# An 8-tap causal convolution on one core: H0 takes over a row sum of H1, and half of an H1 output moves from VectorE to ScalarE and GpSimd

## The chip, the core and the metric

The kernel runs on one core of a Trainium2 chip. The metric is the device time of one execution in microseconds (us). The kernel before takes 728.31 us, the median of three runs (727.57 to 728.33). The execution that the profiler recorded took 728.58 us, and its span, from the first to the last instruction of the program, is 726.8 us; 1.78 us lie around the span.

## The reference

```
out = zeros_like(x)                       # x: (8, 4096, 512), kernel: (8, 512, 512), float32
for k in range(8):
    shifted = x if k == 0 else concat([zeros((B, k, D)), x[:, :-k, :]], axis=1)
    out += matmul(shifted, kernel[k])
```

Each output row is the sum of eight products of 512x512 matrices with the present row of x and the seven before it.

## The kernel before

**Layout.** The 8 x 4096 rows are cut into 128 runs of 256 rows, one run for each partition. A "row" below is one time step t of all 128 runs: a tile of 128 x 512. The first four rows are computed directly; the other 252 are computed in 21 blocks of 12.

**The algorithm.** The eight taps are three bits, and on each bit a product of two 2-part sums is replaced by three products instead of four. So a block has four *nodes*: PL, MI, H1 and H0 (numbers k = 4m+1 to 4m+4 in block m). A node forms sums of rows of x, multiplies them with sums of taps (the W tiles), and gives four output rows in two halves, LO and HI, of two rows each. The outputs of a block are H1's sums (rows t to t+3), the middle sums (t+4 to t+7, out of PL and MI), and H0's (t+8 to t+11).

**The steps of a node**, by the names that the order list uses (the digit after the dot says which node: .0 to .3 are PL, MI, H1 and H0 of the block, .4 to .6 the first three of the next; in s0, s1, v0, v1, d0, d1, F0, F1, e0, e1 the last digit is the half, in l00 to l11 the half and the row):

- z (VectorE): seven sums or differences of rows of XR into Z, 128 x 3584 in one instruction or 1536 + 2048 in two where the ring of 20 rows wraps. H0 takes three of its seven from H1 and computes four (128 x 2048).
- A (VectorE): two sums of neighbouring Z rows (128 x 1024). PL and H1 keep Z in rows 0 to 6 of the tile and their A in rows 9 and 10; MI and H0 keep Z in rows 4 to 10 and their A in rows 0 and 1.
- s (VectorE): five sums of Z rows two apart into S (128 x 2560). F0, F1 (VectorE): two sums each of neighbouring S rows (128 x 1024).
- a1, u, a0 (TensorE): products with A and Z into the PSUM pair q; after a1 ScalarE copies one bank of q onto the other, and a0 waits for that.
- s0, s1 (ScalarE): the seeds, copies of q into the two PSUM pairs p[LO] and p[HI]; dt (ScalarE): a copy of q into DT in SBUF.
- v0, v1 (TensorE): products with S onto the seeds; d0, d1 (VectorE): p[.][0] = DT minus p[.][1] and the like; l00 to l11 (TensorE): products with F onto both rows.
- e0, e1: the ends. For PL two ScalarE instructions, for MI, H1 and H0 one VectorE instruction of 128 x 1024 that reads PSUM and a y tile; H1's and H0's ends are followed by a store. ga, gb (GpSimd): halves of the middle sums, 128 x 512 f32 each, then a store.

Every product is four matmuls of 128 x 128 by 128 x 512, so a block has 36 products, 144 matmuls. The PSUM pairs of p go round by three, the y tiles are five buffers.

**The order of the work** is written out by hand: a prologue line by line (`go`, `do`, `wsum`, ...), then the list ORDER once for each block. Each engine executes its own steps strictly in this order; semaphores keep the dependences between engines. `behind` makes a GpSimd instruction wait for the VectorE instruction that stands last before it in the program; GpSimd also issues the loads of x (r0 to r2), SyncE the transposes into XR (x12, x16, x20) and the stores. LATE places two weight sums of the prologue (wl, wh) at steps of the list.

**Lines.** `tt` records every VectorE tensor_tensor at line 84 and `stt` every scalar_tensor_tensor at line 87; all products have line 125; GpSimd's halves have line 276; the ScalarE copies are lines 186 (q), 202 and 204 (s0, s1), 208 (dt), 247 and 249 (PL's ends). The change touches node_s, node_F, comps, node_e, the ORDER list and LATE.

Of the kernel before, what the change touches and what calls it, by code (L numbers as in the profile page):

```python
# [8 lines left out]
LO, HI, MID = 0, 1, 2  # L9
H1, H0, MI, PL = 0, 1, 2, 3  # L10
# [4 lines left out]
def kernel(  # L15
# [6 lines left out]
    nc = tc.nc  # L22
    B, S, D = x.shape
    K = kernel.shape[0]
    P = 128
# [8 lines left out]
    ADD = mybir.AluOpType.add  # L34
    SUB = mybir.AluOpType.subtract
# [34 lines left out]
    F = spool.tile([P, 4, D], bf, name="F")  # L70
# [12 lines left out]
    def tt(o, a, b, op):  # L83
        last["dve"] = nc.vector.tensor_tensor(out=o, in0=a, in1=b, op=op)  # L84

    def stt(o, a, by, b, op):
        last["dve"] = nc.vector.scalar_tensor_tensor(out=o, in0=a, scalar=by, in1=b, op0=MUL, op1=op)  # L87
# [18 lines left out]
    def load_x(t):  # L106
        if t < RUN:
            xd[t] = dpool.tile([P, 4, D], bf, name="xd")
            return rows(xd[t], t, 4)

    def behind(i):
        tc.add_manual_dep(i.ins, last["dve"].ins.name,
                          mybir.DependencyInfo(mybir.DependencyClass.Sync, mybir.DependencyReason.DATA),
                          reason="behind")

    def transpose_x(t):
        if t < RUN:
            transpose(t, xd[t])
# [10 lines left out]
    class Node:  # L129
        def __init__(self, k, t, a):  # L130
            self.k, self.t, self.a = k, t, a
            self.z, self.o = Z, 4 if a in (MI, H0) else 0
            self.leaf = k in LEAF
            self.s = WX[:, 0:5] if k <= EARLY and k % 2 else S
            if k <= EARLY:
                self.A = WX[:, 5 + 2 * (k % 2):7 + 2 * (k % 2)]
            elif self.o:
                self.A = Z[:, 0:2]
            else:
                self.A = Z[:, 9:11]  # L140
            self.p = {}
# [20 lines left out]
    def node_A(n):  # L162
        tt(n.A, n.z[:, n.o + 2:n.o + 4], n.z[:, n.o + 3:n.o + 5], ADD)

    def node_s(n):
        tt(n.s, n.z[:, n.o:n.o + 5], n.z[:, n.o + 2:n.o + 7], ADD)

    def node_F(n, b_):
        if not n.leaf:
            s = n.s  # L170
            tt(F[:, 2 * b_:2 * b_ + 2], s[:, 2 * b_:2 * b_ + 2], s[:, 2 * b_ + 1:2 * b_ + 3], ADD)

    def comps(n):
        s, a = n.s, n.A
        return (n.z[:, n.o + 3], [a[:, 0], a[:, 1]], [s[:, j] for j in range(5)],
                [F[:, j] for j in range(4)])

    def node_a1(n):
        n.q = pair(3)
        u, a, _, _ = comps(n)  # L180
        if n.leaf:
            product(n.q[:, 1], u, W[n.a, MID, MID], True)
            nc.scalar.mul(out=n.q[:, 0], in_=n.q[:, 1], mul=-1.0)
        else:
            product(n.q[:, 1], a[1], W[n.a, MID, HI], True)
            nc.scalar.copy(out=n.q[:, 0], in_=n.q[:, 1])  # L186

    def node_a0(n):
        product(n.q[:, 0], comps(n)[1][0], W[n.a, MID, LO], False)

    def node_u(n):
        u, a, _, _ = comps(n)
        if n.leaf:
            product(n.q[:, 1], a[1], W[n.a, MID, HI], False)
        else:
            product(n.q[:, 1], u, W[n.a, MID, MID], False)
# [17 lines left out]
    def node_d(n, b_):  # L214
        if n.leaf:
            return
        p = n.p[b_]
        if b_ == LO:
            tt(p[:, 0], DT, p[:, 1], SUB)
        else:  # L220
            stt(p[:, 0], p[:, 1], -1.0, DT, SUB)
# [9 lines left out]
    def store(t, y):  # L231
        nc.sync.dma_start(out=orr[:, t:t + 2, :], in_=y)

    cc, dd = {}, {}

    def y_tile():
        return ypool.tile([P, 2, D], f32, name="y")

    def node_e(n, b_):
        p, t = n.p[b_], n.t + 2 * b_  # L240
        first = n.k <= 4
        if n.a == PL:
            cc[b_] = y_tile()
            if first:
                nc.scalar.mul(out=cc[b_], in_=p, mul=0.5)
            else:
                nc.scalar.copy(out=cc[b_], in_=p)  # L247
                dd[b_] = y_tile()
                nc.scalar.mul(out=dd[b_], in_=cc[b_], mul=-0.5)
        elif n.a == MI:  # L250
            if first:
                dd[b_] = y_tile()
                stt(dd[b_], p, -0.5, cc[b_], ADD)
            else:
                stt(dd[b_], p, 0.5, dd[b_], ADD)
        elif n.a == H1:
            y = y_tile()
            tt(y, p, dd[b_], ADD if first else SUB)
            store(t, y)
        elif n.k == len(nodes) - 1 and b_ == HI:  # L260
            for j, eng in enumerate((nc.scalar, nc.sync)):
                stt(dd[b_][:, j], dd[b_][:, j], -1.0, p[:, j], SUB)
                eng.dma_start(out=orr[:, t + 8 + j, :], in_=dd[b_][:, j])
        else:
            if first:
                tt(dd[b_], dd[b_], p, SUB)
            else:
                stt(dd[b_], dd[b_], -1.0, p, SUB)
            store(t + 8, dd[b_])

    def middle(n, b_):
        stt(cc[b_], cc[b_], 2.0, dd[b_], SUB)
        store(n.t + 4 + 2 * b_, cc[b_])
# [13 lines left out]
    def terms(a, b_, c_):  # L287
        if a == MI and b_ != MID and c_ != MID:
            return W[H0, b_, c_], W[H1, b_, c_]
        if b_ == c_ == MID:  # L290
            return W[a, MID, LO], W[a, MID, HI]
        if b_ == MID:
            return W[a, HI, c_], W[a, LO, c_]
        return W[a, b_, LO], W[a, b_, HI]

    def wsum(a, b_, c_):
        p, m = terms(a, b_, c_)
        tt(W[a, b_, c_], p, m, SUB)
# [51 lines left out]
    def direct_out(b_):  # L350
        y = y_tile()
        nc.scalar.copy(out=y, in_=pd[b_])
        store(2 * b_, y)
# [4 lines left out]
    def s_rows(n, a, b):  # L358
# [2 lines left out]
    nodes = [None] + [Node(1 + 4 * k + i, HEAD + STEP * k, a) for k in range(NB)  # L361
                      for i, a in enumerate((PL, MI, H1, H0))]
    ORDER = """
        d1.1 a0.2 s.2 e0.1 z.3 F0.2 A.3 u.2 l10.1 l11.1 ga0.2 x16.0 x20.1 dt.2 e1.1 s0.2 s1.2 v0.2 v1.2 r1.6
        d0.2 F1.2 d1.2 a1.3 l01.2 a0.3 s.3 z.4 u.3 dt.3 s0.3 l00.2 gb0.2 v0.3 e0.2 l10.2 d0.3 s1.3 F0.3
        l11.2 v1.3 F1.3 l01.3 A.4 s.4 ga1.2 gb1.2 a1.4 l00.3 e1.2 d1.3 e0.3 u.4 a0.4 s1.4 l10.3 z.5 r2.2
        l11.3 s0.4 v0.4 dt.4 v1.4 A.5 a1.5 F0.4 d0.4 r0.2 F1.4 d1.4 l00.4 s.5 e1.3 l01.4 e0.4 a0.5 u.5 s0.5
        z.6 l10.4 s1.5 l11.4 v0.5 F0.5 A.6 v1.5 dt.5 d0.5 a1.6 e1.4 l01.5 x12.4 l00.5 F1.5
    """.split()

    def rows_ahead(n, i):
        d = load_x(n.t + 3 * STEP + 4 * i)
        if d:
            behind(d)

    ACTS = {
        "z": node_z, "s": node_s, "A": node_A, "a1": node_a1, "a0": node_a0, "u": node_u,
        "F0": lambda n: node_F(n, 0), "F1": lambda n: node_F(n, 1),
        "s0": lambda n: node_seed(n, 0), "s1": lambda n: node_seed(n, 1), "dt": node_dts,
        "v0": lambda n: node_v(n, 0), "v1": lambda n: node_v(n, 1),  # L380
# [7 lines left out]
        "x12": lambda n: transpose_x(n.t + 12), "x16": lambda n: transpose_x(n.t + 16),  # L388
        "x20": lambda n: transpose_x(n.t + 20), 
        "r0": lambda n: rows_ahead(n, 0), "r1": lambda n: rows_ahead(n, 1), "r2": lambda n: rows_ahead(n, 2),  # L390
        "wl": lambda n: wsum(H0, LO, MID), "wh": lambda n: wsum(H0, HI, MID),
    }
    AHEAD = {"F0": 1, "s": 1, "z": 2, "A": 2, "a0": 1, "u": 1, "a1": 2, "b1": 1, "s0": 1, "s1": 1,
# [3 lines left out]
    def do(name, k):  # L397
        if k < len(nodes) and (name, k) not in done:
            done.add((name, k))
            ACTS[name](nodes[k])  # L400

    def go(k, name):
        do("a1" if name == "b1" else name, k + AHEAD.get(name, 0))
# [118 lines left out]
    go(3, "v1")  # L522
    node_v(nodes[1], 1)
    node_F(nodes[1], 0)
    direct_out(1)
    node_A(nodes[2])
    node_d(nodes[1], 0)
    go(2, "v0")
    node_a1(nodes[2])
    wsum(MI, MID, LO)  # L530
    wsum(MI, MID, MID)
    load_x(20)
    go(1, "l00")
    node_d(nodes[1], 1)
# [19 lines left out]
    go(1, "v0")  # L554
    go(1, "F0")
    go(2, "a0")
    go(1, "d0")
    go(2, "F1")
    go(2, "u")
# [40 lines left out]
    go(4, "l00")  # L600
    go(3, "s1")
    go(4, "b1")
    wsum(H1, LO, MID)
    go(4, "s")
    go(4, "F0")
    go(4, "l11")
    go(4, "a0")
    go(4, "e0")
    go(4, "u")
# [3 lines left out]
    go(4, "z")  # L613
    go(4, "A")
    go(4, "g1")
    do("r1", 7)
    go(4, "s0")
    go(4, "v0")
    go(4, "d0")
# [5 lines left out]
    done |= {("r0", 3), ("r1", 3), ("r2", 3)}  # L625
    done |= {(name, k) for name in ("ga0", "gb0", "ga1", "gb1") for k in (1, 2, 3, 4)}
    done |= {(name, k) for name in ("F0", "F1", "dt", "v0", "v1", "d0", "d1") for k in LEAF}
    LATE = {(0, "d1.4"): [("wl", 8)], (0, "z.6"): [("wh", 8)]}
    for m in range(NB):
        for token in ORDER:  # L630
            name, i = token.split(".")
            do(name, 4 * m + int(i) + 1)
            for late in LATE.get((m, token), ()):
                do(*late)


# [28 lines left out]
```

## Time and profile before

| what | value |
|---|---|
| median of three runs | 728.31 us |
| the profiled execution, and its span | 728.58 us, 726.8 us |
| TensorE busy (matmuls) | 701.1 us, 96% of the span |
| VectorE busy | 696.9 us, 96% |
| ScalarE busy | 277.3 us, 38% |
| GpSimd busy | 142.7 us, 20% |
| mean granted TensorE clock | 0.997 |
| DMA, mean rate | 192 GB/s |

The page gives busy time and share of each engine, the span in 40 slices, the chain of work that ended last, and groups of equal instructions with the mean duration of one and the idle time before them. Busy time is the union of the instructions' spans. The matmuls are pipelined, and so are VectorE's instructions to a small degree: a record lasts longer than the distance to the next one's start. What an instruction takes from its engine is the distance from its start to the next start, called its *slot* below.

### The profile page before, as it was taken

The page shows a single profiled execution, that of the slowest core. Times are in us where ns is not written, and L with a number is a line of the kernel's source. Part 1 is how long each engine was busy: PE and PEld are TensorE (multiplying, and loading weights), DVE is VectorE, ACT ScalarE, POOL GpSimd, SP SyncE. Part 2 cuts the span into 40 slices and gives each one's busy share as a digit, 9 for nine tenths or more (in the row PEclk, how much of TensorE's full clock was granted, in tenths as well). Part 3 has the DMA queues.
Part 4 walks back from the last instruction along what each step waited for, and adds up shares of the span by engine and source line. Part 5 has one row for each costly group of instructions (what it writes and reads, how often), then busy time and mean ns, then how long its engine had stood idle before and what let it go on. Part 6 is the DMA issues. An engine that isn't in the chain of part 4 may idle for free. (4 is left out here: it accounts for less than half of the span.)

```text
span 726.8 us, 8952 instructions
## 1 busy us (share of the span) xinstructions
PE 701.1 (96%) x3205; PEld 314.9 (43%) x3270; DVE 696.9 (96%) x767; ACT 277.3 (38%) x428; POOL 142.7 (20%) x160
## 2 busy tenths in 40 slices
PE   8989999999999999999999999999999999999996
PEld 3444434444444444444444444444444444444442
DVE  1889999999999999999999999999999999999995
ACT  3043343342525334252533425253342525334251
POOL 4210002113130211313021131202113120211202
PEclk9999999999999999999999999999999999999998
DMA  9999696987969797697969769696986969675324
GB/s 194 210 212 217 180 193 191 195 203 168 240 191 195 200 196 208 161 241 195 190 202 198 199 165 237 200 200 194 195 209 156 233 204 171 193 172 177 98 114 173
DMA packets 161451, 139.38 MB, mean 192 GB/s; under 512 B 132224, under 2 KB 136320, under 8 KB 161280
## 3 DMA queue, kind: packets, MB, share of 16 engines
q1 hardware_dynamic: 147536, 100.42, 49.5%
q0 software_dynamic: 13728, 38.15, 31.2%
q8 instruction: 25, 0.41, 0.2%
q10 hardware_dynamic: 144, 0.26, 0.1%
q14 instruction: 18, 0.15, 0.1%
HBM read 77.33 MB, written 99.09 MB: 243 GB/s over the span
## 5 line engine op out<-in xcount | busy, mean ns | idle before, releaser
L125 PE MATMUL pp<-w,F 128*128 128x512 bf16 x1283 | 313.1, 379 | 1.9 <-DVE pp L84 0.2
L125 PE MATMUL pp<-w,Z 128*128 128x512 bf16 x942 | 231.8, 379 | 2.7 <-DVE Z L84 1.7
L125 PEld LDWEIGHTS <-F 128*128 128x128 bf16 x1312 | 128.2, 98 | 157.9 <-issue 5.4
L276 POOL TENSOR_TENSOR y<-y 128x512 f32<-128x512 f32 x80 | 100.8, 1271 | 439.4 <-DVE Z L84 309.0
L125 PE MATMUL pp<-w,S 128*128 128x512 bf16 x659 | 160.7, 379 | 7.0 <-ACT pp L202 6.2
L84 DVE TENSOR_TENSOR Z<-XR 128x2048 bf16<-128x2048 bf16 (+3 forms) x109 | 154.4, 1434 | 1.2
L125 PEld LDWEIGHTS <-Z 128*128 128x128 bf16 x960 | 92.2, 97 | 117.6 <-DVE Z L84 12.5
L186 ACT COPY pp<-pp 128x512 f32<-128x512 f32 x82 | 46.7, 570 | 224.0 <-PE pp L125 224.0
L84 DVE TENSOR_TENSOR S<-Z 128x2560 bf16<-128x2560 bf16 x81 | 119.9, 1480 | 0.0
L84 DVE TENSOR_TENSOR F<-S 128x1024 bf16<-128x1024 bf16 x160 | 109.1, 683 | 1.0 <-PE pp L125 0.4
L125 PEld LDWEIGHTS <-S 128*128 128x128 bf16 x672 | 65.5, 97 | 89.6 <-issue 14.7
L204 ACT ACTIVATE pp<-pp 128x512 f32<-128x512 f32 (+1 forms) x84 | 49.1, 585 | 84.1 <-DVE y L87 49.0
L208 ACT COPY DT<-pp 128x512 f32<-128x512 f32 x82 | 48.5, 591 | 59.6 <-PE pp L125 59.6
L84 DVE TENSOR_TENSOR pp<-DT,pp 128x512 f32<-128x512 f32 x82 | 56.1, 685 | 2.2 <-PE pp L125 2.2
L93 POOL DMA_DIRECT2D xd<-in_x_dram x61 | 32.2, 528 | 126.1 <-DVE y L87 44.0
L87 DVE SCALAR_TENSOR_TENSOR pp<-pp,DT 128x512 f32<-128x512 f32 x82 | 56.5, 689 | 0.0
L84 DVE TENSOR_TENSOR Z<-Z 128x1024 bf16<-128x1024 bf16 x78 | 53.4, 684 | 0.6
L84 DVE TENSOR_TENSOR y<-pp,y 128x1024 f32<-128x1024 f32 x42 | 51.1, 1216 | 1.4 <-PE pp L125 1.4
L202 ACT COPY pp<-pp 128x512 f32<-128x512 f32 (+1 forms) x84 | 49.8, 593 | 5.5 <-PE pp L125 5.5
L87 DVE SCALAR_TENSOR_TENSOR y<-pp,y 128x1024 f32<-128x1024 f32 x42 | 51.0, 1214 | 0.3 <-PE pp L125 0.3
L247 ACT COPY y<-pp 128x1024 f32<-128x1024 f32 x40 | 40.7, 1018 | 24.9 <-PE pp L125 22.4
L87 DVE SCALAR_TENSOR_TENSOR y<-y,pp 128x1024 f32<-128x1024 f32 (+1 forms) x41 | 48.5, 1184 | 0.8 <-PE pp L125 0.7
(33 smaller groups left out, 213.9 us busy)
## 6 DMA issues: line engine op xcount, KB each, us to landing
out_dram<-y SPq DMA_DIRECT2D x127, 512.0 KB, 3.5
xd<-in_x_dram POOLq DMA_DIRECT2D x61, 512.0 KB, 7.4
w<-in_kernel_dram POOLq DMA_DIRECT2D x8, 512.0 KB, 16.8
w<-in_x_dram SPq DMA_DIRECT2D x1, 1024.0 KB, 4.9
w<-in_x_dram POOLq DMA_DIRECT2D x2, 512.0 KB, 13.9
XR<-xd SPq DMA_TRANSPOSE x62, 5.9
w<-in_x_dram POOLq DMA_DIRECT2D x2, 256.0 KB, 17.8
w<-in_x_dram POOLq DMA_DIRECT2D x1, 384.0 KB, 20.6
```

Of the source, the lines that this page charges most:

```text
L84: last["dve"] = nc.vector.tensor_tensor(out=o, in0=a, in1=b, op=op)
L87: last["dve"] = nc.vector.scalar_tensor_tensor(out=o, in0=a, scalar=by, in1=b, op0=MUL, op1=op)
L93: return nc.gpsimd.dma_start(out=o, in_=src)
L125: nc.tensor.matmul(bank, lhsT=comp[:, c * P:(c + 1) * P], rhs=w[:, c, :], start=start and c == 0, stop=c == DC - 1, skip_group_check=True)
L186: nc.scalar.copy(out=n.q[:, 0], in_=n.q[:, 1])
L202: nc.scalar.copy(out=o, in_=q)
L204: nc.scalar.mul(out=o, in_=q, mul=-1.0)
L208: nc.scalar.copy(out=DT, in_=n.q[:, 0])
L247: nc.scalar.copy(out=cc[b_], in_=p)
L276: behind(nc.gpsimd.tensor_tensor(out=cc[b_][:, j], in0=cc[b_][:, j], in1=dd[b_][:, j], op=ADD))
```

## The change

1. **H0's S row.** For the 20 H0 nodes that are not leaves, node_s computes four rows of S (1 to 4, written to rows 0 to 3 of the tile) and no longer row 0. That row equals row 4 of H1's S, which still lies in row 4 of the tile. F0 of these nodes reads row 0 of the tile twice (a broadcast over the two outputs) and rows 1 and 4 with a stride of three rows; F's two rows come out swapped, and comps gives them to the products in the right order.
2. **H1's first end.** For the 20 H1 nodes after the first block, e0 subtracts one of the two rows on VectorE (128 x 512 in place of 128 x 1024). A new step E0 copies the other row from PSUM to the y tile on ScalarE, a new step ya0 subtracts the y tile dd from it on GpSimd, behind VectorE's last instruction, and stores both rows.
3. **The order.** ORDER is another list: the same steps and E0.2 and ya0.2, cut at another place (the list now begins with l10.0). In the prologue three weight sums stand earlier, two loads of x move by some steps, and wl, wh and a load (r2) are placed by LATE at other steps.

```diff
+            self.shares = a == H0 and not self.leaf
     def node_s(n):
-        tt(n.s, n.z[:, n.o:n.o + 5], n.z[:, n.o + 2:n.o + 7], ADD)
+        if n.shares:
+            tt(n.s[:, 0:4], n.z[:, n.o + 1:n.o + 5], n.z[:, n.o + 3:n.o + 7], ADD)
+        else:
+            tt(n.s, n.z[:, n.o:n.o + 5], n.z[:, n.o + 2:n.o + 7], ADD)
     def node_F(n, b_):
...
+        s, f = n.s, F[:, 2 * b_:2 * b_ + 2]
+        if not n.shares:
+            tt(f, s[:, 2 * b_:2 * b_ + 2], s[:, 2 * b_ + 1:2 * b_ + 3], ADD)
+        elif b_ == LO:
+            tt(f, s[:, 0:1].to_broadcast([P, 2, D]), s[:, 1:5:3], ADD)
+        else:
+            tt(f, s[:, 1:3], s[:, 2:4], ADD)
     def comps(n):
+        si, fi = ((4, 0, 1, 2, 3), (1, 0, 2, 3)) if n.shares else (range(5), range(4))
...
         elif n.a == H1:
-            y = y_tile()
-            tt(y, p, dd[b_], ADD if first else SUB)
-            store(t, y)
+            yy[b_] = yy.get(b_) or y_tile()
+            if first or b_ == HI:
+                tt(yy[b_], p, dd[b_], ADD if first else SUB)
+                store(t, yy.pop(b_))
+            else:
+                tt(yy[b_][:, 0], p[:, 0], dd[b_][:, 0], SUB)
+    def node_E(n):
+        if n.a == H1 and n.k > 4:
+            yy[LO] = yy.get(LO) or y_tile()
+            nc.scalar.copy(out=yy[LO][:, 1], in_=n.p[LO][:, 1])
+    def node_y(n):
+        if n.a == H1 and n.k > 4:
+            y = yy.pop(LO)
+            behind(nc.gpsimd.tensor_tensor(out=y[:, 1], in0=y[:, 1], in1=dd[LO][:, 1], op=SUB))
+            store(n.t, y)
...
     ORDER = """
+        l10.0 s0.1 x12.0 l11.0 A.2 v0.1 dt.1 s1.1 v1.1 F0.1 d0.1 a1.2 F1.1 l00.1 l01.1 a0.2 r1.6 u.2 d1.1
+        s.2 e0.1 e1.0 s1.2 s0.2 l10.1 l11.1 dt.2 z.3 F0.2 v0.2 v1.2 A.3 F1.2 ga0.2 a1.3 x16.0 d0.2 l01.2
+        x20.1 e1.1 s.3 l00.2 gb0.2 a0.3 u.3 r0.6 d1.2 r2.6 s0.3 e0.2 z.4 F0.3 A.4 l11.2 l10.2 v0.3 F1.3 E0.2
+        dt.3 ya0.2 s1.3 v1.3 d0.3 a1.4 e1.2 l00.3 s.4 gb1.2 l01.3 d1.3 a0.4 u.4 e0.3 s0.4 z.5 F0.4 dt.4 s1.4
+        l10.3 l11.3 A.5 ga1.2 v0.4 v1.4 d0.4 a1.5 l01.4 d1.4 l00.4 a0.5 e0.4 F1.4 e1.3 s.5 u.5 z.6
...
+    wsum(MI, MID, LO)
+    wsum(MI, MID, MID)
     node_d(nodes[1], 0)
     go(2, "v0")
     node_a1(nodes[2])
-    wsum(MI, MID, LO)
-    wsum(MI, MID, MID)
...
+    wsum(H1, LO, MID)
     go(1, "d0")
...
-    LATE = {(0, "d1.4"): [("wl", 8)], (0, "z.6"): [("wh", 8)]}
+    LATE = {(0, "F1.4"): [("wl", 8)], (1, "A.2"): [("wh", 8)], (1, "u.2"): [("r2", 7)]}
```

The 3270 matmuls, the 74 DMAs that GpSimd issues and SyncE's transposes and stores are the same in number; ScalarE gets 20 copies more, GpSimd 20 subtractions more. VectorE has as many instructions as before, 40 of them shorter.

More of the change, by code (lines that the diff above doesn't have):

```diff
@@ L165, in node_s @@
     def node_s(n):
-        tt(n.s, n.z[:, n.o:n.o + 5], n.z[:, n.o + 2:n.o + 7], ADD)
+        if n.shares:
+            tt(n.s[:, 0:4], n.z[:, n.o + 1:n.o + 5], n.z[:, n.o + 3:n.o + 7], ADD)
+        else:
+            tt(n.s, n.z[:, n.o:n.o + 5], n.z[:, n.o + 2:n.o + 7], ADD)
     def node_F(n, b_):
-        if not n.leaf:
-            s = n.s
-            tt(F[:, 2 * b_:2 * b_ + 2], s[:, 2 * b_:2 * b_ + 2], s[:, 2 * b_ + 1:2 * b_ + 3], ADD)
+        if n.leaf:
+            return
+        s, f = n.s, F[:, 2 * b_:2 * b_ + 2]
[5 more added lines that the diff above has]
+            tt(f, s[:, 1:3], s[:, 2:4], ADD)
     def comps(n):
         s, a = n.s, n.A
-        return (n.z[:, n.o + 3], [a[:, 0], a[:, 1]], [s[:, j] for j in range(5)],
-                [F[:, j] for j in range(4)])
+        si, fi = ((4, 0, 1, 2, 3), (1, 0, 2, 3)) if n.shares else (range(5), range(4))
+        return (n.z[:, n.o + 3], [a[:, 0], a[:, 1]], [s[:, j] for j in si], [F[:, j] for j in fi])
     def node_a1(n):
@@ L232, in store @@
         nc.sync.dma_start(out=orr[:, t:t + 2, :], in_=y)
-    cc, dd = {}, {}
+    cc, dd, yy = {}, {}, {}
     def y_tile():
@@ L363 @@
     ORDER = """
[L364 to L368, printed above, removed]
+        l10.0 s0.1 x12.0 l11.0 A.2 v0.1 dt.1 s1.1 v1.1 F0.1 d0.1 a1.2 F1.1 l00.1 l01.1 a0.2 r1.6 u.2 d1.1
[3 more added lines that the diff above has]
+        l10.3 l11.3 A.5 ga1.2 v0.4 v1.4 d0.4 a1.5 l01.4 d1.4 l00.4 a0.5 e0.4 F1.4 e1.3 s.5 u.5 z.6
     """.split()
@@ L390 @@
         "r0": lambda n: rows_ahead(n, 0), "r1": lambda n: rows_ahead(n, 1), "r2": lambda n: rows_ahead(n, 2),
+        "E0": node_E, "ya0": node_y,
         "wl": lambda n: wsum(H0, LO, MID), "wh": lambda n: wsum(H0, HI, MID),
@@ L602 @@
     go(4, "b1")
-    wsum(H1, LO, MID)
+    do("r0", 7)
     go(4, "s")
@@ L606 @@
     go(4, "l11")
+    do("r1", 7)
     go(4, "a0")
@@ L615 @@
     go(4, "g1")
-    do("r1", 7)
     go(4, "s0")
@@ L631 @@
             name, i = token.split(".")
-            do(name, 4 * m + int(i) + 1)
-            for late in LATE.get((m, token), ()):
+            if m or name[0] != "r":
+                do(name, 4 * m + int(i) + 1)
+            for late in LATE.pop((m, token), ()):
                 do(*late)
+    assert not LATE
 _INS = ['x', 'kernel']
```

## The prediction

> **What bounds the kernel now.** The page comes first: two engines are busy 96% of the span, and in the 40 slices both read 9 from the third slice to the last but one. So a mean does not tell which of them waits for the other; the steady part has to be cut out.
>
> ```profile
> PE 701.1 (96%) x3205; PEld 314.9 (43%) x3270; DVE 696.9 (96%) x767; ACT 277.3 (38%) x428; POOL 142.7 (20%) x160
> ```
>
> In the timeline each block has one short stall of TensorE behind a seed (line 202). It marks the period: 331.78 - 300.01 = 31.77 us.
>
> ```profile
> 300.01 1.02 PE L125 MATMUL pp<-w,S 128*128 128x512 bf16 x4 [0.30 <-ACT pp L202]
> ...
> 331.78 1.02 PE L125 MATMUL pp<-w,S 128*128 128x512 bf16 x3 [0.30 <-ACT pp L202]
> ```
>
> The view by windows over 19 such periods (109.42 to 713.07 us; after the length come PE, PEld, DVE, ACT, POOL):
>
> ```profile
> 109.42:713.07 603.65, 594.42 (x2681) 265.71 (x2736) 599.98 (x669) 239.94 (x380) 123.04 (x126) 1.00 0.78 189
> ```
>
> The reader is to see three things. Weight loads are 2736 = 19 x 144, so every product is in. VectorE is busy 599.98 of 603.65: 31.58 of 31.77 us a period, and its idle 0.19 is the sum of a dependence of A on the z just ahead (0.1) and a short wait for a product. TensorE's matmuls start 0.2157 us apart when nothing stops them (in the timeline 8 of them take 1.73 from group to group), so a period's 144 need 31.06 us, and 0.71 us of each is lost. The waits say that VectorE has hardly anything to wait for, and TensorE only the seeds:
>
> ```profile
> PE pp L125 <- ACT pp L202: 7.0, 21, 0.7
> DVE pp L84 <- PE pp L125: 2.2, 2, 2.1
> ```
>
> **VectorE sets the period**, TensorE follows 2% below it. The stall at the seed is only where TensorE's slack shows. Hence the gain has a ceiling: 19 x 0.71 = 13.5 us in these periods, however much VectorE sheds.
>
> **What the change takes from VectorE.** The rows by form:
>
> ```profile
> L84 DVE TENSOR_TENSOR S<-Z 128x2560 bf16<-128x2560 bf16 x81 | 119.9, 1480 | 0.0
> L84 DVE TENSOR_TENSOR F<-S 128x1024 bf16<-128x1024 bf16 x160 | 109.1, 683 | 1.0 <-PE pp L125 0.4
> L84 DVE TENSOR_TENSOR Z<-XR 128x2048 bf16<-128x2048 bf16 x45 | 54.6, 1214 | 0.0
> L84 DVE TENSOR_TENSOR pp<-DT,pp 128x512 f32<-128x512 f32 x82 | 56.1, 685 | 2.2 <-PE pp L125 2.2
> L84 DVE TENSOR_TENSOR y<-pp,y 128x1024 f32<-128x1024 f32 x42 | 51.1, 1216 | 1.4 <-PE pp L125 1.4
> L276 POOL TENSOR_TENSOR y<-y 128x512 f32<-128x512 f32 x80 | 100.8, 1271 | 439.4 <-DVE Z L84 309.0 <-issue 78.4 <-ACT pp L204 35.5
> ```
>
> - H0's S shrinks from 2560 to 2048 elements; the 2048 row (1214) stands for it: -0.27 us.
> - H1's first end shrinks from 1024 to 512 f32 elements with one operand in PSUM, like the row pp<-DT,pp: 1216 - 685 = -0.53 us.
> - H0's F0 reads a broadcast and a strided operand. No row shows that form. Its ends: 0 (as the F row, slot 0.60) and +0.53 (unpacked, as the 1216 row, slot 1.13). I take 0, since it is bf16 with contiguous rows of 512, nearest to the F row. [...]
>
> Together -0.80 a period: VectorE needs 30.78 busy, about 30.9 with the dependence of A on z (now A.2 behind z.6). That is below 31.06: **TensorE becomes the bound**, and the question is what it still waits for.
>
> **What is late next.** I laid the new list out over one period: 36 products at 0.863 us, VectorE's slots (0.60 for A, F, d and the half end; 1.13 for 2048 bf16 and 1024 f32; 1.40 for S; 1.94 for z of 3584, 2.01 for z in two pieces), ScalarE's slots 0.48. An instruction that waits for a product starts about 0.20 after that product's slot (the last end at 720.33, its product's slot over at 720.08; ScalarE's at 108.30 after 108.09); a product that waits for Z starts 0.24 after the VectorE end, the weight load between (A over at 304.09, load 304.15, matmul 304.33).
>
> - The d steps now sit where they fit: each has 1.73 us between the end of its v product and its l product, and needs 0.20 + 0.69 + 0.24. No stall.
> - One loop is longer than TensorE's. z.4 overwrites the Z rows 0 and 1 that hold H0's A, so it waits for product a0.3. From there VectorE does z.4 1.94, F0.3, A.4, F1.3, d0.3 4 x 0.60, e1.2 1.13, s.4 1.40, d1.3 0.60, e0.3 1.13, z.5 1.94, F0.4 0.60, A.5 0.69 = 11.83, and then a1.5 may start: 0.20 + 11.83 + 0.24 = 12.27. TensorE has 14 products between a0.3 and a1.5: 12.08. So it stalls 0.19 at a1.5, and 0.33 in two blocks of five where both z come in two pieces: 0.25 on average. Elsewhere VectorE now waits for TensorE (before d0.2, e0.1, z.4).
> - ScalarE: E0.2 (a copy like DT's, 0.59) stands between s0.3 and dt.3, s1.3. Product u.3 ends at 15.53 of the period, s0.3 starts at 15.74, s1.3 ends at 17.8, v1.3 starts at 18.12: hidden, with 0.3 in hand; without that cover a slot of 0.48 a block. The seeds now stand ahead of dt at s1.2, s0.2 and s0.3, so the 0.30 wait at v0.3 goes; its 0.46 (with restart) is not a gain of its own, it is part of the 0.71. E0 also waits for e0.2 (at 14.0) and for the y buffer's store, some 10 us old.
> - GpSimd: 6.4 us of subtractions a period in place of 5.1. ya0.2 waits for F1.3 and ends at about 20.2; e0.3, which overwrites its operand dd, comes at 22.3, and the y buffer is asked for at 29.6. Hidden.
> - GpSimd beside VectorE. In this trace each of the 80 subtractions lies beside VectorE instructions with one operand in PSUM, never beside z, A, s or F. In the new list two do not: gb0.2 (behind s.3, 1.27 long) has only d1.2 and e0.2 (1.19) before z.4, and ga1.2 (behind A.5) only d0.4 and d1.4 before F1.4. What an overlap costs no row shows: between 0 and, if the later one waits until the earlier one ends, 0.25 to 0.4 us each. I take 0.05 a period: z.4 waits for a0.3 until almost that time anyway, and F1.4 lies behind A.5, where VectorE has about 0.3 in hand. [...]
> - SyncE: x12.0 and x16.0 still wait for z.6 and land 5.9 us later, against z.4 13 us on; the middle stores keep about their places. The loads r0 to r2 run blocks ahead. No cost.
>
> **Start.** The two sums (MI, MID, .) move into an idle time of VectorE, but TensorE has no gap from 56 to 96 us, so that buys little; and the stall below, which waits for an A, is taken over by d0.1 a step later, since wh now stands between A.2 and F0.1. I take -0.2 there (0 to -1.5), and -0.3 for the seed stall at 109.
>
> ```profile
> 51.09 0.70 DVE L84 TENSOR_TENSOR pp<-DT,pp 128x512 f32<-128x512 f32 x1 [2.07 <-PE pp L125]
> 96.85 1.04 PE L125 MATMUL pp<-w,Z 128*128 128x512 bf16 x4 [1.67 <-DVE Z L84]
> ```
>
> **End.** The last end waits here for the last product:
>
> ```profile
> 716.77 2.49 POOL L276 TENSOR_TENSOR y<-y 128x512 f32<-128x512 f32 x2 [4.01 <-issue]
> 720.33 1.28 DVE L87 SCALAR_TENSOR_TENSOR y<-y,pp 128x512 f32<-128x512 f32 x2 [0.66 <-PE pp L125]
> ```
>
> In the new list ga1.2 comes behind e0.3, and the last end overwrites its operand: e0.3's end + 0.1 + 1.27 is some 0.9 later than the last product allows. The last stores bunch up too. Against that the last block loses a shorter stall (0.3). Net +0.5 (0 to +1.2).
>
> **The sum**, against the profiled execution: a period 31.06 + 0.25 + 0.05 + 0.02 = 31.38 for 31.77; 19 x -0.39 = -7.4. Start -0.5, end +0.5. Span 726.8 - 7.4 = 719.4, the run 728.58 - 7.4 = **721.2 us**; that execution lies 0.27 over the median of the runs.
>
> **Rivals.**
> 1. *GpSimd and VectorE exclude each other* and both new overlaps cost: z.4 and F1.4 late by 0.25 to 0.4 each. The first is in TensorE's loop, the second partly absorbed: 0.15 to 0.25 more a period, 724 to 726. For it: the trace keeps the two apart without exception; against it: nothing measured.
> 2. *Another wait takes the place*: a slip of my table by one slot (a d step or s1.3 too late by 0.4) costs 19 x 0.4 = 7.6 and the time is 728.5. For it: all windows are 0.2 to 0.5 wide; against it: VectorE has some 0.2 to 0.3 us a period to catch up.
> 3. *Slower: F0 runs unpacked.* F0.3 stands in the loop from z.4 to a1.5: +0.53 there makes the period 31.06 + 0.32 + 0.53 = 31.91, 0.14 over before: 19 x 0.14 + 0.5 - 0.5 = +2.7, 731. It decides from 0.39 us a block on. For it: the form is new; against it: its rows are contiguous.
> 4. *The order does better*, overlaps and loop cost nothing (the last product's wait shorter, z.5 early): 31.17 a period, 717.
>
> **Chances.** The forecast's case (717.5 to 723.5) 0.50; rival 1 (to 726.5) 0.17; rival 2 0.10; rival 3 and other slower mishaps 0.17; rival 4 0.06. A measurement of this kernel can tell 0.2% (1.5 us) from no change. Faster by more than that: 0.50 + 0.17 + 0.06 = 0.73; the same 0.10; slower 0.17. The range 717.5 to 728 leaves out rival 4's lower part and the slower cases, 0.2 in all.
>
> **What would show it.** Period 31.3 to 31.5 between like products; VectorE's idle up from 0.19 to 0.5 or more a period and ended by PE; S 128x2048 near 1214, the half end near 685, F0 near 683 (over 1000: rival 3); one TensorE stall a block, of 0.2 to 0.4, at a product with Z ended by VectorE (a1.5), none behind line 202's successor; z.4 or F1.4 starting at the end of a GpSimd subtraction is rival 1; the last VectorE instruction ended by POOL. Wrong would be a VectorE that stays busy 99% with the period near 31.8, or a TensorE stall at an l product or a seed.

## The result, and the profile after

The changed kernel takes **741.04 us** (median of six runs, 734.03 to 750.75) where the kernel before takes 728.32: the ratio is 1.0139 [1.0119, 1.0160], slower by 1.4%. Its lowest run lies above the highest of before (728.92). (Ratios here and below leave out runs over 1.5% above the fastest of their kernel, here 747.97 and 750.75; medians and ranges take in all.) The profiled execution took 740.49 us, with a span of 738.7.

Read in the order of the prediction. First the page of the changed kernel: busy time, then two rows of the 40 slices.

```profile
PE 702.9 (95%) x3205; PEld 317.0 (43%) x3270; DVE 684.7 (93%) x767; ACT 285.5 (39%) x448; POOL 167.7 (23%) x180
...
DVE  1999969879999999999999699999999999999994
...
PEclk9999989999999999999999899999999999999998
```

VectorE is busy 684.7 us where it was 696.9, so the work did go away. But its row has holes, and TensorE's granted clock dips beside them. Between the holes the kernel is quick. The windows view, over six periods without a hole (columns as in the prediction: length, PE, PEld, DVE, ACT, POOL, granted clock, DMA share, GB/s):

```profile
184.24:371.19 186.95, 185.91 (x848) 84.09 (x864) 186.01 (x213) 78.06 (x126) 47.26 (x49) 1.00 0.86 203
```

That is 31.16 us a period, against 31.77 before and 31.38 forecast. Now the same view between two marks, the same z early in the steady part and 19 periods later, in the kernel before and then in the changed one:

```profile
101.04:704.67 603.63, 594.45 (x2684) 265.69 (x2737) 601.26 (x669) 239.94 (x380) 122.31 (x126) 1.00 0.80 192
```

```profile
106.33:715.41 609.08, 591.97 (x2666) 266.25 (x2721) 589.51 (x668) 246.14 (x396) 144.51 (x142) 0.99 0.79 189
```

The first mark comes 5.3 us later, the 19 periods take 609.08 instead of 603.63, and what follows the second mark 23.3 instead of 22.1. The waits of the changed kernel (total, times, longest) name what fills the holes; before had none of the first two rows:

```profile
DVE y L84 <- DMA out_dram<-y: 10.4, 3, 5.1
DVE Z L84 <- DMA XR<-xd: 9.1, 2, 6.1
```

```profile
PE pp L125 <- DVE pp L87: 8.6, 3, 4.5
PE pp L125 <- DVE Z L84: 8.3, 4, 5.2
```

**One such hole, engine by engine.** e1.2 writes into a y buffer whose earlier content, cc0, must first be stored; gb0.2 on GpSimd ends cc0 and SyncE issues the store. In this order below: GpSimd, SyncE, VectorE and TensorE of the changed kernel, from the timelines.

```profile
401.12 1.27 POOL L300 TENSOR_TENSOR y<-y 128x512 f32<-128x512 f32 x1 [1.44 <-DVE S L84]
402.34 1.04 POOL L93 DMA_DIRECT2D xd<-in_x_dram  x2
```

```profile
389.61 13.37 SPq L100 DMA_TRANSPOSE XR<-xd  x3
403.08 0.52 SPq L242 DMA_DIRECT2D out_dram<-y  x1
```

```profile
406.30 0.69 DVE L84 TENSOR_TENSOR pp<-DT,pp 128x512 f32<-128x512 f32 x1
412.11 1.22 DVE L84 TENSOR_TENSOR y<-pp,y 128x1024 f32<-128x1024 f32 x1 [5.12 <-DMA out_dram<-y]
```

```profile
408.99 1.89 PE L125 MATMUL pp<-w,Z 128*128 128x512 bf16 x8
415.39 3.57 PE L125 MATMUL pp<-w,F 128*128 128x512 bf16 x8 [4.51 <-DVE pp L87]
```

gb0.2 is done at 402.39. But SyncE is held in the issue of its third transpose until 402.98 and issues the store only at 403.08, after both x loads (402.34 and 402.87). The store lands 8.9 us later. In the block before, where SyncE was free (store at 371.28, between its two loads at 371.19 and 371.7), it landed in 3.7 us, and e1.2, at 375.54, had 0.58 us in hand. The landing of the two stores, first that of 371.28, then that of 403.08:

```profile
DMA to landing us min/median/max: 3.7/3.7/3.7
DMA to landing us min/median/max: 8.9/8.9/8.9
```

Here e1.2 waits 5.12 us, TensorE stands for 4.51, and when it starts again 8 matmuls take 3.57 us instead of 1.89. The windows show why; the third figure from the end is the granted clock:

```profile
371.00:402.00 31.00, 30.84 (x142) 13.99 (x144) 30.77 (x35) 13.01 (x21) 7.72 (x9) 1.00 0.87 187
402.00:413.00 11.00, 8.82 (x41) 3.92 (x40) 5.73 (x8) 2.62 (x5) 2.64 (x4) 1.00 1.02 236
413.00:420.00 7.00, 4.61 (x11) 1.62 (x11) 6.66 (x8) 1.74 (x3) 1.53 (x2) 0.52 0.37 151
```

The clock records hold 0.5 for 6.83 us there, from 413.23, as they do from 106.03, and for 3.41 us from 160.64. TensorE's stops before them last 4.51, 5.19 and 3.31 us; the half clock begins 2.35, 2.40 and 4.04 us after the last matmul before the stop, in the third case when TensorE is at work again (since 159.91). What sets its beginning and its length is not shown.

The three waits of e1.2 are not all of this kind. Those of 5.12 us and 3.69 us (at 156.6) follow a store behind both loads (8.9 and 8.3 us), with a late transpose still under way as well. In the third, 1.58 us, the store of 564.95 stands between its two loads as usual and yet takes 5.85 us. A transpose is on its way beside it until 567.67, but beside the store of 309.00, which takes 3.9, one is too; the cause stays open.

### The profile page after: what moved, and what is told of

It is laid out like the page before. It is cut to its first block, busy times and chain, and to the rows that moved or that the text cites. A ratio compares the mean times of both kernels' runs of the same rounds, so it can differ in the third digit from the quotient of the medians.

```text
span 738.7 us, 8999 instructions
## 1 busy us (share of the span) xinstructions
PE 702.9 (95%) x3205; PEld 317.0 (43%) x3270; DVE 684.7 (93%) x767; ACT 285.5 (39%) x448; POOL 167.7 (23%) x180
## 4 chain that ended last, share of the span: by engine, by line
PE 71%; DVE 13%; DMA 6%; issue 3%; SPq 1%; ACT 0%; POOLq 0%; POOL 0%; DVEq 0%
PE pp L125 71%; DVE Z L84 4%; DMA XR<-xd 4%; DMA out_dram<-y 2%; DVE S L84 2%; DVE y L87 2%; DVE F L84 1%; DVE y L84 1%; DVE w L84 1%; DVE pp L87 1%; SPq L100 0%; DVE pp L84 0%; POOLq L688 0%; POOL y L300 0%; ACT y L255 0%
## 5 line engine op out<-in xcount | busy, mean ns | idle before, releaser
L300 POOL TENSOR_TENSOR y<-y 128x512 f32<-128x512 f32 x80 | 101.6, 1270 | 292.8 <-DVE F L84 138.0
L125 PE MATMUL pp<-w,S 128*128 128x512 bf16 x658 | 158.9, 381 | 0.7
L84 DVE TENSOR_TENSOR S<-Z 128x2560 bf16<-128x2560 bf16 (+1 forms) x81 | 114.5, 1414 | 0.0
L84 DVE TENSOR_TENSOR F<-S 128x1024 bf16<-128x1024 bf16 x160 | 111.0, 693 | 1.9 <-PE pp L125 1.9
L214 ACT ACTIVATE pp<-pp 128x512 f32<-128x512 f32 (+1 forms) x84 | 51.0, 607 | 22.0 <-PE pp L125 14.5
L87 DVE SCALAR_TENSOR_TENSOR pp<-pp,DT 128x512 f32<-128x512 f32 x82 | 56.6, 690 | 0.7 <-PE pp L125 0.5
L87 DVE SCALAR_TENSOR_TENSOR y<-pp,y 128x1024 f32<-128x1024 f32 x42 | 51.1, 1216 | 0.5 <-PE pp L125 0.5
L84 DVE TENSOR_TENSOR y<-pp,y 128x1024 f32<-128x1024 f32 (+1 forms) x42 | 40.3, 960 | 11.1 <-DMA out_dram<-y 10.4
L87 DVE SCALAR_TENSOR_TENSOR y<-y,pp 128x1024 f32<-128x1024 f32 (+1 forms) x41 | 48.4, 1183 | 1.7 <-POOL y L300 1.4
## 6 DMA issues: line engine op xcount, KB each, us to landing
w<-in_x_dram POOLq DMA_DIRECT2D x2, 512.0 KB, 13.4
```

The costliest lines, as they stand in the source:

```text
L125: nc.tensor.matmul(bank, lhsT=comp[:, c * P:(c + 1) * P], rhs=w[:, c, :], start=start and c == 0, stop=c == DC - 1, skip_group_check=True)
L214: nc.scalar.mul(out=o, in_=q, mul=-1.0)
L300: behind(nc.gpsimd.tensor_tensor(out=cc[b_][:, j], in0=cc[b_][:, j], in1=dd[b_][:, j], op=ADD))
```

## The experiments

Times are medians; the ratio is to the kernel before, run on the same chip. Three chips were used, on which before took 727.64 (the first four rows), 727.49 (loads_apart to old_loads_beside) and 727.84.

| kernel | us (range) | ratio |
|---|---|---|
| loads_moved | 720.91 (720.56 to 722.64) | 0.9908 [0.9889, 0.9926] |
| pair_moved | 728.34 (723.89 to 741.46) | 0.9998 [0.9965, 1.0031] |
| r1_moved | 771.80 (771.07 to 774.23) | 1.0607 [1.0586, 1.0628] |
| pair_ahead | 814.74 (805.97 to 818.26) | 1.1151 [1.1077, 1.1225] |
| loads_apart | **716.53** (716.49 to 717.60) | 0.9853 [0.9838, 0.9867] |
| order_only | 728.45 (728.17 to 729.30) | 1.0011 [1.0002, 1.0020] |
| share_old_order | 727.72 (727.22 to 728.57) | 1.0004 [0.9994, 1.0013] |
| old_loads_beside | 730.96 (729.78 to 732.19) | 1.0046 [1.0029, 1.0063] |
| apart_share_only | 723.35 (723.34 to 723.42) | 0.9933 [0.9915, 0.9951] |
| apart_half_only | 720.73 (720.58 to 722.09) | 0.9901 [0.9884, 0.9919] |
| apart_start_of_after | 723.19 (722.26 to 724.00) | 0.9930 [0.9912, 0.9949] |
| store_first | 725.73 (723.21 to 741.47) | 0.9957 [0.9934, 0.9979] |

### Is it where the loads stand?

**loads_moved** moves three tokens of the list and thins the loads at the start.

```diff
- a0.2 r1.6 u.2 ... x20.1 e1.1 s.3 ... u.3 r0.6 d1.2 r2.6 s0.3 ... e1.2 l00.3 ... d1.3 a0.4
+ a0.2 u.2 ... x20.1 e1.1 r1.6 s.3 ... u.3 d1.2 s0.3 ... e1.2 r0.2 l00.3 ... d1.3 r2.2 a0.4
-    do("r0", 7)                                  # at the start; r1.7 goes back behind g1
-    LATE = {..., (1, "u.2"): [("r2", 7)]}
```

> The changed kernel with its loads of x (DRAM to DRAM, by GpSimd's queue) in other places: the two loads that stood beside gb0.2 come behind e1.2 and d1.3, the third comes behind e1.1 instead of between the transposes, and the start loads one block less ahead. Nothing else is changed. Theory A (the loads beside the transposes and beside the store that e1.2's y buffer waits for make these land late; a late landing stops VectorE, then TensorE, and a stop of over 3 us is followed by 3.4 to 6.8 us at half the granted clock): the waits of VectorE for a DMA (10.4 and 9.1 us in the changed kernel's trace) and the stretches at half clock go, the period is the 31.16 of its undisturbed blocks, so 728.6 - 19 x 0.61 = 717, 715 to 720. Theory B (the new order leaves the y buffer and the transposes too little room wherever the loads stand): stops stay, 730 to 745.

Measured 720.91: theory B falls. It is 1 us above A's range: the moved third load now stands 2.2 us ahead of the store of cc0, which takes 4.2 to 4.4 us in most blocks and leaves e1.2 nothing in hand (waits of 1.1 and 0.9 us in two blocks).

**pair_moved** moves only the two loads beside gb0.2, **r1_moved** only the third.

```diff
  pair_moved
- u.3 r0.6 d1.2 r2.6 s0.3 ... e1.2 l00.3 s.4 gb1.2 l01.3 d1.3 a0.4
+ u.3 d1.2 s0.3 ... e1.2 r0.6 l00.3 s.4 gb1.2 l01.3 d1.3 r2.6 a0.4
  r1_moved
- a0.2 r1.6 u.2 d1.1 ... x20.1 e1.1 s.3
+ a0.2 u.2 d1.1 ... x20.1 e1.1 r1.6 s.3
```

> The changed kernel with only the pair of loads beside gb0.2 moved behind e1.2 and d1.3; the third load stays between the transposes, the start is as in the changed kernel. Theory A: e1.2 has no wait for the store any more (10.4 us of VectorE in the trace, and some 5 us of what half the clock costs behind two of them), the waits of z for transposes at about 106 and 148 us stay: 740.5 - 15 = 725, 720 to 731. Theory B: e1.2 goes on waiting, 734 to 750. If the third load alone holds the store up (theory C: a transpose that lands late holds SyncE, and the store behind it is issued late), e1.2 still waits in a block or two, but the store then lands in 2.6 to 4 us and the wait is under 1 us.

> The changed kernel with only the third load moved, from between the transposes x16 and x20 to behind e1.1; the pair beside gb0.2 stays. Theory C (the chain begins at this load: the transpose beside it takes 10 to 13 us in place of 5, SyncE is held until it lands, the store behind it is issued behind both loads of the pair in place of between them and lands in 8.3 to 8.9 us in place of 3.7): the transposes land in 5 to 7 us, the store is issued within 0.1 us of the end of gb0.2 in every block, and e1.2 waits nowhere or once; at the start only the stop at 106 us is left: 720 to 728. If the pair does it by itself, e1.2 goes on waiting in some blocks: 732 to 745.

In pair_moved e1.2 never waits for a store again, as A said; C had left a short wait in a block or two. What is left is z, waiting for a transpose beside the third load, and it varies from run to run (723.89 to 733.37 in nine of the ten). Its worst case, from VectorE's timeline:

```profile
275.23 2.03 DVE L84 TENSOR_TENSOR Z<-XR 128x3584 bf16<-128x3584 bf16 x1 [7.66 <-DMA XR<-xd]
```

The transpose was issued at 257.0, the load 0.7 us behind it; both landed at 275.1, 18 us later.

r1_moved is a clear miss of mine. Half of theory C holds: the transposes of the steady part land in 4.2 to 6.6 us, and the store is issued 0.03 us after gb0.2 ends in every block. But the store now lies behind one load that is 2.2 us old and behind the first of the pair, and takes 5.7 to 8.5 us, so e1.2 waits in every block that loads. The waits of r1_moved:

```profile
DVE y L84 <- DMA out_dram<-y: 42.8, 16, 3.7
```

So SyncE's lateness is one way into the trouble, not the trouble itself. That is how many loads stand ahead of the store.

**pair_ahead** puts the pair just ahead of gb0.2.

```diff
- l00.2 gb0.2 a0.3 u.3 r0.6 d1.2 r2.6 s0.3
+ l00.2 r0.6 r2.6 gb0.2 a0.3 u.3 d1.2 s0.3
```

> The changed kernel with the pair of loads just ahead of gb0.2 on GpSimd instead of just behind it: the same bytes, about 1.3 us earlier, and the store of cc0 is always issued behind both. Theories A and C: the store takes 8.3 to 8.9 us (as where it came behind both loads) instead of 3.7, less the 1.3 or so that the loads are ahead, so e1.2 is 2.5 to 4.5 us late in each of some 15 blocks, and behind stops of over 3 us the clock is halved for 3.4 to 6.8 us: 15 x (2.5 to 4.5 + 0 to 2.5) over 725, 765 to 830. Theory B: the place of the loads is of no weight, 735 to 750.

814.74. The same bytes, about a microsecond earlier, cost 74 us more than in the changed kernel. The loads now stand 2.4 and 1.8 us ahead of the store in 15 of 16 blocks, mostly with no transpose under way, and it lands in 7.2 to 9.4 us (14.2 in the other, where SyncE is late too). Not all of the 74 is the store's: gb0.2 has to wait for the issue of the loads and falls beside z.4, which then takes 1.2 us longer, in all some 16 us of VectorE (point 3 below). The waits of pair_ahead:

```profile
DVE y L84 <- DMA out_dram<-y: 66.2, 16, 9.6
```

**store_first** leaves every load in its place and lets GpSimd issue that store, ahead of the pair.

```diff
-            store(n.t + 4 + 2 * b_, cc[b_])
+            t = n.t + 4 + 2 * b_
+            (nc.sync if b_ else nc.gpsimd).dma_start(out=orr[:, t:t + 2, :], in_=cc[b_])
```

> The changed kernel with all loads where it has them; only the store of cc0 behind gb0.2 is issued by GpSimd instead of SyncE, so that it always stands ahead of the pair of loads and does not wait for SyncE. If the order of issue decides (theory D), the store lands in 2.6 to 4 us in every block and e1.2's long waits for it (10.4 us, and the half clock behind them) go; z still waits for transposes beside the third load, as in pair_moved: 722 to 732. If it is the load on the DMA engines whatever was issued first, the store takes 6 us or more and e1.2 is late by 2 or more in each block: 755 to 800.

725.73. The store lands in 3.0 us (median of the instruction view; 2.9 to 5.2), and e1.2 waits for it in one block, by 0.2 us. The two blocks with a transpose and the third load late, as at 403 us above, have it land in 4.9 and 5.2. Of DMA waits in VectorE's steady part only z's remain:

```profile
DVE Z L84 <- DMA XR<-xd: 7.1, 4, 4.6
```

The loads stand in the list where the changed kernel has them, so it is not their bytes but the order of issue that decides. Two more things differ here, and this run does not part them from the order: the store goes by GpSimd's queue, and the loads start about a microsecond later.

**loads_apart** puts the third load behind z.4, when the store of cc0 is already on its way.

```diff
- x20.1 e1.1 r1.6 s.3 ... e0.2 z.4 F0.3            # as in loads_moved
+ x20.1 e1.1 s.3 ... e0.2 z.4 r1.6 F0.3
```

> As loads_moved, but the third load comes behind z.4 (after the store of cc0 is issued) instead of behind e1.1, where it was 2.2 us ahead of that store. Theory D (e1.2 has only some 4.3 us from the store's issue, and the store lands in 2.6 us with no load beside it, in 3.7 to 4.4 with one, in 6.6 to 8.9 with two or three): the store lands in 2.6 to 2.9 us and e1.2 has 1.3 us or more in hand in every block, none of its waits of up to 1.1 us is left, the period goes from 31.29 (loads_moved) to 31.1: 720.9 - 16 x 0.19 = 717.9, 716 to 719.5. Theory B' (the rest of the loss in loads_moved is the order's own): 720 to 722.

716.53: theory D. The store lands in 2.6 us and e1.2 has 1.4 to 1.7 us in hand (3.6 and 0.8 in one block), and VectorE waits for no DMA of the steady part. This version beats both kernels. Between the two marks:

```profile
99.94:691.89 591.95, 588.95 (x2683) 265.94 (x2735) 588.66 (x669) 247.20 (x399) 146.67 (x145) 1.00 0.79 195
```

591.95 / 19 = 31.16 us a period, the period of the changed kernel's undisturbed blocks; the clock is 1.00 throughout and the DMA share is that of the changed kernel, 0.79. The DMA engines carry as much; it only stands apart.

**apart_start_of_after** is loads_apart with the changed kernel's loads at the start.

```diff
+    do("r0", 7)                                  # and r1.7, r2.7 early, as in the changed kernel
- r0.2 ... r2.2
+ r0.6 ... r2.6
```

> loads_apart with the start's loads as the changed kernel has them (three more loads of x before 115 us, one block further ahead); in the steady part the loads stand apart. It prices the start alone: the transposes before the first steady block go beside loads again, z waits 4 to 6 us for them at about 105 us, TensorE stops for 3.3 to 5.2 and may lose 1.7 to 3.4 more to half the clock: 716.5 + 3.5 to 8 = 720 to 724.5. If the start's loads do not matter, 716 to 718.

723.19, 6.7 us more: TensorE stands for 4.61 us until 108.8 and then has 3.4 us of half clock. It agrees with the marks: the changed kernel reaches the first one 6.4 us after loads_apart (106.33 and 99.94).

**old_loads_beside** turns it round: the kernel before, with its loads where the changed kernel has them.

```diff
- x16.0 x20.1 ... v1.2 r1.6 d0.2 ... gb0.2 v0.3 ... z.5 r2.2 ... d0.4 r0.2 F1.4
+ x16.0 r1.6 x20.1 ... v1.2 d0.2 ... gb0.2 r0.2 r2.2 v0.3 ... z.5 ... d0.4 F1.4
```

> The kernel before, operations and order unchanged, with its loads of x put where the changed kernel has them: two just behind gb0.2, the third between the transposes x16 and x20. In the trace of before this store lands in 2.63 us and e1.2 has 0.9 us in hand. Theory D: with a load on either side the store takes 3.7 to 4 us, 0.2 to 0.4 too much in each block, which TensorE's 0.7 us of slack partly hides; where SyncE is still in the transposes' issue the store falls behind both loads and takes 8 to 9, with a stop of 3.5 to 5 us and a stretch at half clock: 0 to 8 such blocks, 728 to 765, likeliest 735 to 745. Theory B (only the new order has too little room): 727 to 730.

730.96, 3.5 us slower: the cause is there in the old order too, but mildly. The store takes 3.5 to 4.1 us where it took 2.63, and e1.2 waits by up to 0.6 in six blocks. SyncE is never late here, so the 8 us case does not come up, and my likeliest value (735 to 745) was too high. The third load stands between x16 and x20 in the list, but is issued only behind the third transpose (167.67 and 165.15 in one block), so the run tests the pair and not a load beside the transposes.

```profile
DVE y L84 <- DMA out_dram<-y: 2.3, 6, 0.6
```

### What are order and operations worth without the loads?

**order_only** is loads_apart without the two shed operations; **apart_share_only** and **apart_half_only** have one of them each; **share_old_order** is the kernel before with the S share alone.

```diff
  order_only: both; apart_half_only: the first; apart_share_only: the last three
-            self.shares = a == H0 and not self.leaf
+            self.shares = False
-            if first or b_ == HI:                # in node_e
+            if True:
-        if n.a == H1 and n.k > 4:                # in node_E and node_y
+        if False:
  share_old_order, in the kernel before: the changed kernel's shares, node_s, node_F and comps
```

> loads_apart with the old operations: H0's S whole on VectorE (2560 elements, no shared row, F as before), H1's first end whole on VectorE, no copy on ScalarE and no extra subtraction on GpSimd; the list's order and the loads stay. If the two shed operations are worth what their rows say (0.27 + 0.53 us of VectorE a period), VectorE is busy 31.58 again and bounds the kernel: 31.7 to 31.9 a period, 727 to 731, about the kernel before. If the order itself carried the gain, 717 to 722.

> The kernel before, order and loads unchanged, with only the share of the S row (S of H0 2560 to 2048 elements, F of H0 from a broadcast and a strided operand). The rows of the changed kernel give S 1214 in place of 1480 and F 685 as before: 0.27 us of VectorE a period, 20 x 0.27 = 5.4, 728 - 5.4 = 722.5, 721 to 724.5, since TensorE (31.06) is still below 31.5. If the order of before has no use for it (TensorE's waits stay where they are), 727 to 729.

> loads_apart with the S row's share and without the half end (H1's first end whole on VectorE, no copy on ScalarE, no extra subtraction on GpSimd). If in this order each 0.27 us shed from VectorE counts until TensorE bounds: from order_only's 728.45, 19 x 0.27 = 5.1 less, 723.3, 722 to 725. If the share is worth nothing by itself, as in the old order (share_old_order 727.7 against 727.5), 727 to 729.

> loads_apart with the half end and without the S row's share. VectorE sheds 0.53 us a period: from order_only's 31.84 to some 31.3, near TensorE's 31.06: 728.45 - 19 x 0.53 = 718.4, 717.5 to 720. If the two edits only work together, 724 or more.

The new order by itself is worth nothing (728.45), and so is the share in the old order (727.72, a miss). Together they pay (the single ones ran on another chip than order_only, so the differences hold to some 0.4 us): the share takes 728.45 - 723.35 = 5.1 us in the new order, 19 x 0.27, as its row says. The half end takes 7.7, which is 19 x 0.41 and not 0.53: my 718.4 was 2.3 too low. (Only with the half end does z.4 come so early that it overlaps gb0.2, which takes back 0.1; see point 3 below.) Both take 11.9, where the two add up to 12.8.

Why the old order has no use for 0.27 us of VectorE is in the waits of share_old_order:

```profile
DVE F L84 <- PE pp L125: 5.5, 19, 0.4
```

```profile
PE pp L125 <- ACT pp L212: 7.0, 21, 0.7
```

VectorE now waits for TensorE once a block, by 5.5 / 19 = 0.29 us: all that it shed. TensorE's wait at the seed is 7.0 us as before, and the period stays 31.77. So it was not VectorE's work alone that set the old period. The waits point to a loop through TensorE, ScalarE's seed and VectorE that does not contain H0's S, beside a VectorE that was just as full; no run breaks that loop, so which one it is is not shown.

## Why the prediction was wrong, point by point

The spans against that of the kernel before, part by part:

| part | forecast | changed kernel | loads_apart |
|---|---|---|---|
| up to the first mark | -0.5 | +5.3 | -1.1 |
| 19 periods | -7.4 | +5.4 | -11.7 |
| behind the second mark | +0.5 | +1.2 | +0.8 |
| span | -7.4 | +11.9 | -12.0 |

1. **The step that failed** is the one on SyncE: "the middle stores keep about their places. The loads r0 to r2 run blocks ahead. No cost." I asked when the loads' own data is needed, and not what stands beside them while they run. They cost 609.08 - 591.95 = 17.1 us in the periods and 6.4 at the start; nearly all of the 24 us between the changed kernel and loads_apart. The kernel before showed the narrow place. Its store of the same cc0 is issued at 301.85 and lands in 2.6 us, its e1.2 starts 0.9 us after that, and its loads stand well clear of both (one at 295.46, landed by then, the next at 310.59). GpSimd's timeline of before, the store, its landing and e1.2:

```profile
300.56 1.27 POOL L276 TENSOR_TENSOR y<-y 128x512 f32<-128x512 f32 x1 [4.56 <-DVE Z L84]
...
310.59 0.54 POOL L93 DMA_DIRECT2D xd<-in_x_dram  x1 [2.37 <-DVE Z L84]
312.52 0.52 POOL L93 DMA_DIRECT2D xd<-in_x_dram  x1 [1.39 <-DVE pp L84]
...
327.26 0.54 POOL L93 DMA_DIRECT2D xd<-in_x_dram  x1
```

```profile
301.85 0.81 SPq L232 DMA_DIRECT2D out_dram<-y  x2
DMA to landing us min/median/max: 2.6/2.6/2.6
305.42 1.22 DVE L84 TENSOR_TENSOR y<-pp,y 128x1024 f32<-128x1024 f32 x1
```

The new list puts two loads against that very store. The order itself gives e1.2 more room, 4.26 us from the store's issue to its start (371.28 and 375.54) where it had 3.57. Of the y buffers I priced the half end's, not the one of e1.2.

2. **What the change takes from VectorE**: the rows were right. S 128x2048 is 1212 ns (1214 forecast), the half end 678 (685), F0 about 0.68 us; rival 3 (F0 as long as the 1216 row) is out. The changed kernel by form:

```profile
L84 DVE TENSOR_TENSOR F<-S 128x1024 bf16<-128x1024 bf16 x160 | 111.0, 693 | 1.9 <-PE pp L125 1.9
...
L84 DVE TENSOR_TENSOR S<-Z 128x2048 bf16<-128x2048 bf16 x20 | 24.2, 1212 | 0.0
L84 DVE TENSOR_TENSOR y<-pp,y 128x512 f32<-128x512 f32 x20 | 13.6, 678 | 0.8 <-PE pp L125 0.8
```

3. **GpSimd beside VectorE** (rival 1): seen, and small because the overlaps are short. F1.4 beside ga1.2 takes 0.78 us instead of 0.68 in all the blocks where they overlap by 0.23; that is what lifts the mean of F to 693. A z of 3584 elements that overlaps gb0.2 by as much takes 2.11 (apart_half_only) instead of 2.01 (order_only); in the changed kernel the two overlap by 0.05 to 0.11 in all blocks but one, and z loses next to nothing. I had put 0.05 a period, with 0.25 to 0.4 each as the upper end; it is 0.10, for F1.4 alone. The overlaps of pair_ahead are long: beside the whole of gb0.2 (1.29 us) the z of 3584 takes 3.25 us, 1.23 more. So in these three cases the loss was the overlap less some 0.1 us (0.10 of 0.23 twice, 1.23 of 1.29; why is not shown), and pair_ahead, where the two overlap in full, paid rival 1's price and more. F1.4 in the changed kernel, then gb0.2 and z.4 in pair_ahead:

```profile
353.05 0.78 DVE L84 TENSOR_TENSOR F<-S 128x1024 bf16<-128x1024 bf16 x1
```

```profile
220.91 1.29 POOL L300 TENSOR_TENSOR y<-y 128x512 f32<-128x512 f32 x1
220.84 3.25 DVE L84 TENSOR_TENSOR Z<-XR 128x3584 bf16<-128x3584 bf16 x1
```

4. **The period**: 31.38 forecast, 31.16 measured without the loads' stops. The 0.25 that I gave to the loop from z.4 to a1.5 hardly shows: loads_apart is 0.10 above TensorE's 31.06. It was rival 4's period (31.17) that came true.

5. **What bounds the kernel now** was half right. That VectorE alone set the period before is refuted by share_old_order. (The two engines read 9 from the fourth of the 40 slices on, not the third.) The period of the new order came to 0.10 of TensorE's 31.06, as said; but VectorE is busy 588.66 of 591.95 there, idle 0.17 a period and not the 0.5 that was to show it, so which of the two bounds loads_apart is not shown. Of the saving in VectorE's busy time, 0.71 a period is there (602.13 in order_only and 588.66 in loads_apart, over 19) where the rows sum to 0.80.

6. **Start and end**: -1.1 and +0.8 in loads_apart, against -0.5 and +0.5; the last end does wait for GpSimd ("DVE y L87 <- POOL y L300", 1.4 us).

7. **The rivals**: rival 2 named "another wait takes the place", but as a slip of my table of engines by 0.4 us, priced at no gain. None of my cases held a transfer that comes late, nor what a stop of TensorE costs on top in clock.

## What to carry to other kernels

When a list is reordered, look for each buffer's last transfer before it is reused, read from the old profile how little room it has (here 0.9 us), and then see which other transfers the new order issues within a few microseconds ahead of it, on any queue. A load that is needed much later should start when nothing urgent is in flight: here the same loads moved by a few tokens make 741, 815 or 717 us. And price a stop of TensorE of 2 us or more with the stretch at half clock that may follow (here 3.4 to 10.2 us).

## What the runs showed of the hardware

- **A 512 KB store's landing went by what was issued ahead of it.** For the store of cc0: mostly 2.6 us with no load of x near it; 3.5 to 4.1 with one 0.1 us ahead and the next 0.44 us behind (once 5.85); 4.2 to 4.5 with one 2.2 us ahead (twice over 5); 5.7 to 8.5 with one 2.2 and one 0.1 us ahead (r1_moved); 7.2 to 9.4 with two some 2 us ahead (pair_ahead); 8.3 and 8.9 with two ahead (by 2.6 and 2.1, and by 0.7 and 0.2 us) and a transpose under way. In pair_ahead the store lands 0.2 to 1.4 us behind the second load in 15 of 16 blocks, in the two late cases of the changed kernel within 0.1 us of it (156.53 and 156.54, 412.01 and 411.94). Why is not settled.
- **A transpose with a load issued 0.6 to 0.8 us behind it landed late, and together with it**: 148.31 and 148.49, 403.26 and 403.33 in the changed kernel, where all eight such transposes of its steady part take 9.2 to 13.4 us and land within 0.25 us of the load; 18 us in pair_moved. A transpose with no load under way beside it takes 4.2 to 6.2 (4.7 in the median) in the kernel before and in the changed one. SyncE was held in the issue of one transpose until the transpose before it had all but landed (until 402.98 for a landing at 403.26, until 367.82 for one at 368.2; in some cases longer), so what was queued behind, a store too, was late as well (issued at 403.08, 0.69 us after gb0.2's end).
- **Half clock came in steps of 3.4 us** (3.4, 6.8, once 10.2). In the changed kernel it followed the stops of TensorE of 5.19, 3.31 and 4.51 us (6.83, 3.41 and 6.83 us) and not the one of 2.17. Over the profiles, 14 of 16 stops of 3.3 us or more have such a stretch, and about half of those of 2.0 to 3.2 us (8 of 15).
